# Where retention's weights begin in memory, and which raw tiles the pooling weights and the last gate rows take

## The chip, the core and the metric

The kernel runs on one core of a Trainium2 chip. The metric is the device time of one execution in microseconds (us). Three executions before the change took 2145.18, 2144.27 and 2141.74 us; the median is 2144.27 us.

The engines are named as the profile names them: PE is TensorE (PEld its loads of weights), DVE is VectorE, ACT is ScalarE, POOL is GpSimd, and SP is SyncE, which issues all but a few of this kernel's DMAs. A matrix product on PE has a stationary operand, the weights (128 columns loaded by one PEld instruction), and a moving operand that streams past them; the result goes to an accumulation bank.

## What is computed

One encoder layer on 1024 tokens of width 1024, in fp32: a SwiGLU block, a gated mixing layer, a second SwiGLU block. The change lies in the mixing layer:

```python
proj = rmsnorm(h) @ w_in            # q | k | v | g_ret | p_pool | gates
q, k = rotary(q), rotary(k) * 256 ** -0.5        # 4 heads of 256
scores = einsum("bnchd,bnshd->bnhcs", qc, kc) * inner_decay   # inside a chunk
inner  = einsum("bnhcs,bnshe->bnche", scores, vc)
cross  = (q_i * q_decay) @ state
state  = state * chunk_decay + (k_i * k_decay).T @ v_i
pooled = trailing_means(p) - p                   # windows 2, 4, 8, 16, one per group
mixed  = einsum("bsgc,gcd->bsgd", pooled, pool_w) * pool_scale
merged = sigmoid(gate0) * (ret @ w_ret_up) + sigmoid(gate1) * (mixed @ w_pool_up)
h = h + merged @ w_out
```

## The kernel before

**Products.** Every fp32 number is split into a high and a low part (`split`, L159: a CAST on ACT at L161 writes the high part, a TENSOR_TENSOR on DVE at L162 the low one; `split_scaled`, L164, does the same with a scale, at L165 and L166). A product is three matrix instructions (`mm3`, L179): high by high (L181), high by low (L182), low by high (L183). So PE runs in triples of lines L181, L182, L183. Most products stream 512 columns; the ones of retention stream 256.

**Order.** `Flow.run` (L62) calls `prep` of a step four steps ahead of its `body`, so loads and splits are written four steps ahead of the products that need them. A scheduler then orders the instructions of each engine by readiness and priority (`with soon()` raises it) and gives every tile a place in its ring; a tile that takes the place of an older one waits until that one has been read for the last time. Each engine, and SP as well, works off its own list in order: an instruction that waits holds up all behind it. The rings that matter here: `mv` (28 places of 4 KB per partition, split operands), `t4` (9 of 4 KB, long-lived tiles), `raw` (4 of 4 KB, weights as they come from memory), `c2` (8 of 2 KB, small results).

**Where weights begin.** `weights` writes the split weights into a `wt` tile (L111) that is 64 elements longer than needed, from element `at` on. The two SwiGLU blocks and the projections have one kind of product that streams 256 columns, that of two groups with blocks in common (`common`, L546); its weights are written from element `APART` = 22 on (L51, L553), which is byte 88 of 256, since tiles start at multiples of 256 bytes. All other weights begin at byte 0 of 256, those of retention too.

**Retention** works in 8 units of one head and one half of the tokens (`Unit`, L1455), named by two digits: unit 21 is head 2, second half. The stages and their names in a trace:

- `loads`: v, q, k from memory. `operands` splits q and k. For the last head `turn` rotates q and k on DVE just ahead.
- `keys` (`by_token`, L1432): PE turns the keys by token (transposes into a bank `kd..b`), and ACT and DVE scale and split them into `kd`, a tile of two parts per 256 tokens.
- `scores` (L1519): q by k into `s`, then DVE masks and scales into `sc`, and the split goes to `sm`.
- `updates`: `st` <- v by `kd`: the turned keys are the weights. Every unit with first half has two updates, with second half one.
- `products`: `ob` <- v by `sm` (`inner`, weights are the masked scores) and `ob` <- state by q (`across`, weights are q).
- `outputs`, `normalise`, `finish`: sums, scaling, PE turns the outputs (`ot`) and DVE multiplies them by the gate (`rg`); `ret` goes to memory.

**Fillers.** Between the stages of the units stand steps of the other branch, so that PE has work: `pool` (L1379) for the four groups, and `pool_up` (L1407) for eight blocks of 48 products of 512 columns. `pool` loads a group's weights into the first half of a raw tile (`pw`), splits them, and multiplies the pooled rows `pl` into `px`; the results are split into `po`. `pool_up` loads its weights into `pu..raw`, and at `begin` a row of gates into a raw tile `pg`; at the end DVE multiplies the bank by the gates in that tile (L1419) and SP stores it as `pm`. In the ring of raw tiles the loads therefore stand pu0raw, pg0, pu1raw, pg1 up to pu7raw, pg7, and then come those of the next stage.

**The next stage** (`merge`) begins with the product by w_ret_up in Strassen form, in pairs of groups: ru0 and ru1 first. A group loads two raw tiles, `ra` and `rb`; sums of their blocks (S1, S2 and so on; L455 on DVE) are split to weights `ru1wS` and multiplied by sums of `ret` (`ruR`, `ruT`). ru0a, ru1a, ru0b, ru1b are the groups' banks.

Of the kernel before, what the change touches and what calls it, by code (L numbers as in the profile page):

```python
# [17 lines left out]
P = 128  # L18
# [72 lines left out]
def block_kernel(ctx: ExitStack, tc, x, x_tok, vecs, f1_in, f1_out, w_in, w_v, pool_w, w_ret, w_pool, w_o,  # L91
# [28 lines left out]
    def raw(name):  # L120
        return sb.tile([P, S], F32, tag="raw", bufs=N_RAW, name=name)
# [17 lines left out]
    def load(dst, src):  # L139
        nc.sync.dma_start(dst, src)  # L140
# [8 lines left out]
    def half(t, j):  # L149
        return t[:, j * H : (j + 1) * H]  # L150
# [34 lines left out]
    def parts(m, at=slice(None)):  # L185
        return m[:, 0, at], m[:, 1, at]
# [1184 lines left out]
    def pooled_rows(n, i, first=False):  # L1371
# [4 lines left out]
        load(r, pooled[2 * n + i])  # L1376
        early[n, i] = [operand(half(r, j), f"{name}{j}") for j in range(2)]

    def pool(n):  # L1379
        Mg, w = {}, []  # L1380

        def prep():
            for i in range(2):
                if (n, i) not in early:
                    pooled_rows(n, i)
                Mg[i] = early[n, i]
            r = raw(f"pw{n}")
            load(half(r, 0), pool_w[n])
            w.append(weights(half(r, 0), f"pw{n}"))

        def body():
            for i in range(2):
                mt = 2 * n + i
                dst = [f(f"px{mt}{j}") for j, f in enumerate((sum_bank, bank))]
                for kt in range(2):
                    for j in range(2):
                        mm3(dst[j], parts(w[0], 2 * kt + i), parts(Mg[kt][j]), kt == 0, kt == 1)
                M[mt] = []
                for j in range(2):
                    m = mv(f"po{mt}{j}")  # L1400
                    with soon():
                        split_scaled(m[:, 0], m[:, 1], dst[j], vec[:, V_SCALE + mt : V_SCALE + mt + 1])
                    M[mt].append(m)

        return prep, body

    def pool_up():  # L1407
        gate = {}
        for mt in range(KT):

            def begin(mt=mt):
                gate[mt] = raw(f"pg{mt}")
                await_stored(f"t{(KT + mt) // 2}")
                load(gate[mt], gates[KT + mt])

            def evac(dst, mt=mt):
                gt = gate.pop(mt)
                for j in range(2):
                    tt(half(gt, j), dst[j], half(gt, j), MUL)  # L1419
                load(pm[mt], gt)  # L1420

            yield from plain(M.get, KT, w_pool[mt], f"pu{mt}", evac, begin,
                             (sum_bank, sum_bank if mt < 4 else bank))
# [5 lines left out]
        yield from pool_up()  # L1429


    def by_token(get, scale, name, n=2):  # L1432

        slots = []
        for jj in range(n):
            b = bank(f"{name}b{jj}")
            m = mv(f"{name}{jj}")
            for z in range(2):
                for i in range(2):
                    j = 2 * jj + z  # L1440
                    nc.tensor.transpose(b[:, z * HD + i * P : z * HD + (i + 1) * P], get(i)[:, j * P : (j + 1) * P],
                                        ident)
            for z in range(2):
                sl = slice(z * HD, (z + 1) * HD)
                with soon():
                    split_scaled(m[:, 0, sl], m[:, 1, sl], b[:, sl], scale(2 * jj + z))
            slots.append(m)
        return slots

    def col(t, n):  # L1450
# [2 lines left out]
    class Unit:  # L1453
# [65 lines left out]
        def scores(self):  # L1519

            self.sm = []
            for j in range(2):
                wid = SPAN - j * P
                b = bank(f"s{self.name}{j}")
                for s in range(2):
                    at, to = s * SPAN + j * P, b[:, s * SPAN : (s + 1) * SPAN]
                    for i in range(2):
                        w, m = parts(self.K[i], slice(at, at + P)), self.Q[i][:, :, at : at + wid]
                        first, final = s == 0 and i == 0, i == 1
                        if j == 0:  # L1530
                            mm3(to, w, (m[:, 0], m[:, 1]), first, final)
                        else:
                            mm(to, w[0], m, start=first, stop=False, skip_group_check=True)
                            mm(to[:, :P], w[1], m[:, 0], start=False, stop=final, skip_group_check=True)
                n = 2 * wid
                c = c2(f"sc{self.name}{j}")
                m = sb.tile([P, 2, H], F32R, tag="t4", bufs=N_T4, name=f"sm{self.name}{j}")
                with soon():
                    src = b
                    if j:  # L1540
                        both, src = b.rearrange("p (s z c) -> p s z c", s=2, z=2), c
                        sums = c[:, :n].rearrange("p (s c) -> p s c", s=2)
# [5 lines left out]
                    split(m[:, 0, :n], m[:, 1, :n], c[:, :n])  # L1548
                self.sm.append(m)

        def cell(self, b, t):
# [13 lines left out]
        def inner(self, s):  # L1565
            b, first = self.into(s)
            for j, t in ((0, 0), (0, 1), (1, 1)):
                at = s * (SPAN - j * P) + (t - j) * P

                mm3(self.cell(b, t), parts(self.sm[j], slice(at, at + P)), self.v(2 * s + j), first and t == 0, j == t)  # L1570

        def update(self, s):

            b = bank(f"st{self.name}{s}")
            for i in range(2):
                for j in range(2):
                    o = j * HD + i * P
                    mm3(b[:, i * HD : (i + 1) * HD], parts(self.kd[s], slice(o, o + P)), self.v(2 * s + j),
                        i == 0 and j == 0, j == 1)
# [410 lines left out]
```

## Time and profile before

| | |
|---|---|
| median of three executions | 2144.27 us |
| profiled execution, its own time | 2143.71 us |
| its span, first to last instruction | 2141.8 us |
| PE busy | 2129.9 us, 99% |
| PEld busy | 1809.6 us, 84% |
| DVE busy | 1874.0 us, 87% |
| ACT busy | 1103.3 us, 52% |
| granted TensorE clock | 1.0 in the whole span |

The profiled execution lies 0.56 us below the median; 1.9 us of its time are outside the span. Busy time is a sum over stages: what a change is worth has to be read in the stage where it acts, from which wait ends last there. A PE instruction's duration overlaps the next one's (they are pipelined), so what a matrix instruction costs PE is the distance from its start to the next start. For a wait the list of instructions in order of time shows the idle time ahead of an instruction in square brackets, with what ended it.

### The profile page before, as it was taken

How to read it: one execution, taken by the hardware profiler on the slowest of the kernel's cores; microseconds unless marked ns; L12 is line 12 of the kernel's file. 1: busy time of each engine (PE TensorE's matmuls, PEld its weight loads, DVE VectorE, ACT ScalarE, POOL GpSimd, SP SyncE). 2: the span in 40 equal slices, each digit the busy share in tenths (PEclk: the TensorE clock that was granted, in tenths of full speed). 3: DMA queues.
4: the chain of work that ended last, by engine and by line, in shares of the span. 5: the costliest groups of instructions: out<-in, count | busy, mean ns of one | idle time of the engine just before them, and what ended most of it. 6: DMA issues, size and time to landing. Idle time of an engine off the chain costs nothing.

```text
span 2141.8 us, 30121 instructions
## 1 busy us (share of the span) xinstructions
PE 2129.9 (99%) x10798; PEld 1809.6 (84%) x10798; DVE 1874.0 (87%) x3352; ACT 1103.3 (52%) x2082; POOL 0.2 (0%) x4
## 2 busy tenths in 40 slices
PE   9999999999999999999999999999999999999998
PEld 7888888888888888888888998788888888888887
DVE  8798898997986799999988888899988978899796
ACT  8544444554644544544457753456644544455454
POOL 0000000000000000000000000000000000000000
PEclk9999999999999999999999999999999999999999
DMA  7232323585543333233336567624133232358542
GB/s 259 75 133 74 138 84 130 200 275 178 173 142 94 109 121 115 106 122 109 119 128 227 196 203 262 220 89 163 64 105 117 90 123 84 131 199 275 192 138 99
DMA packets 116101, 313.59 MB, mean 146 GB/s; under 512 B 12784, under 2 KB 17008, under 8 KB 115952
## 3 DMA queue, kind: packets, MB, share of 16 engines
q1 hardware_dynamic: 115376, 310.63, 42.6%
q8 instruction: 84, 1.38, 0.3%
q10 hardware_dynamic: 576, 1.05, 0.1%
q14 instruction: 65, 0.53, 0.1%
HBM read 220.93 MB, written 90.70 MB: 145 GB/s over the span
## 4 chain that ended last, share of the span: by engine, by line
PE 91%; DVE 6%; DMA 1%; ACT 1%; issue 1%; SPq 0%; ACTq 0%; DVEq 0%
PE a_b L181 2%; PE a_b L182 2%; PE a_b L183 2%; PE c_b L181 2%; PE c_b L182 2%; PE c_b L183 2%; PE c_e L182 2%; PE c_e L181 2%; PE c_e L183 2%; PE a_e L181 2%; PE a_e L182 2%; PE a_e L183 2%; PE a_a L181 1%; PE a_a L183 1%; PE a_a L182 1%; PE c_a L181 1%
## 5 line engine op out<-in xcount | busy, mean ns | idle before, releaser
L182 PE MATMUL c_b<-n3T,c_wS 128*128 128x512 f32 x176 | 68.6, 390 | 0.0
L183 PE MATMUL c_b<-n3T,c_wS 128*128 128x512 f32 x176 | 68.5, 389 | 0.0
L181 PE MATMUL c_b<-n3T,c_wS 128*128 128x512 f32 x176 | 68.4, 390 | 0.0
L182 PE MATMUL a_b<-n1T,a_wS 128*128 128x512 f32 x168 | 65.4, 389 | 0.0
L181 PE MATMUL a_b<-n1T,a_wS 128*128 128x512 f32 x168 | 65.4, 389 | 0.0
L183 PE MATMUL a_b<-n1T,a_wS 128*128 128x512 f32 x168 | 65.3, 389 | 0.0
L181 PE MATMUL a_a<-n1R,a_wL 128*128 128x512 f32 x120 | 46.7, 389 | 0.0
L182 PE MATMUL a_a<-n1R,a_wL 128*128 128x512 f32 x120 | 46.7, 389 | 0.0
L183 PE MATMUL a_a<-n1R,a_wL 128*128 128x512 f32 x120 | 46.7, 389 | 0.0
L182 PE MATMUL c_a<-n3R,c_wL 128*128 128x512 f32 x112 | 43.6, 389 | 0.0
L181 PE MATMUL c_a<-n3R,c_wL 128*128 128x512 f32 x112 | 43.6, 389 | 0.0
L183 PE MATMUL c_a<-n3R,c_wL 128*128 128x512 f32 x112 | 43.6, 389 | 0.0
L183 PEld LDWEIGHTS c_b<-n3T,c_wS 128*128 128x128 f32 x176 | 33.0, 188 | 6.9
L182 PEld LDWEIGHTS c_b<-n3T,c_wS 128*128 128x128 f32 x176 | 33.0, 188 | 6.8 <-DVE n3T L162 0.2
L181 PEld LDWEIGHTS c_b<-n3T,c_wS 128*128 128x128 f32 x176 | 32.9, 188 | 6.9 <-ACT n3T L161 0.3
L162 DVE TENSOR_TENSOR a_wS<-a_S,a_wS 128x512 fp32r<-128x512 f32 x45 | 31.2, 695 | 8.0 <-ACT a_wS L161 8.0
L183 PEld LDWEIGHTS a_b<-n1T,a_wS 128*128 128x128 f32 x168 | 31.5, 188 | 6.6
L181 PEld LDWEIGHTS a_b<-n1T,a_wS 128*128 128x128 f32 x168 | 31.5, 188 | 6.4
L182 PEld LDWEIGHTS a_b<-n1T,a_wS 128*128 128x128 f32 x168 | 31.5, 188 | 6.4
L182 PE MATMUL c_e<-n3T,c_wL 128*128 128x512 f32 x88 | 34.5, 394 | 0.0
L161 ACT CAST c_wS<-c_S 128x512 fp32r<-128x512 f32 x46 | 28.0, 626 | 12.7 <-DVE c_S L455 7.1
L181 PE MATMUL c_e<-n3T,c_wS 128*128 128x512 f32 x88 | 34.4, 391 | 0.0
(3385 smaller groups left out, 8168.5 us busy)
## 6 DMA issues: line engine op xcount, KB each, us to landing
c_ra<-in_f_in SPq DMA_DIRECT2D x22, 512.0 KB, 3.7
c_rb<-in_f_in SPq DMA_DIRECT2D x22, 512.0 KB, 3.7
a_ra<-in_f_in SPq DMA_DIRECT2D x21, 512.0 KB, 3.8
a_rb<-in_f_in SPq DMA_DIRECT2D x21, 512.0 KB, 3.8
t<-au SPq DMA_DIRECT2D x11, 512.0 KB, 2.9
b<-ag SPq DMA_DIRECT2D x11, 512.0 KB, 4.1
r<-au SPq DMA_DIRECT2D x11, 512.0 KB, 3.8
bra<-in_f_out SPq DMA_DIRECT2D x11, 512.0 KB, 5.9
```

Source lines behind the costliest of these rows:

```text
L161: copy(hi, src)
L162: tt(lo, src, hi.bitcast(F32), SUB)
L181: mm(dst, w[0], m[0], start=start, stop=False, skip_group_check=True)
L182: mm(dst, w[0], m[1], start=False, stop=False, skip_group_check=True)
L183: mm(dst, w[1], m[0], start=False, stop=stop, skip_group_check=True)
```

## The change

Three edits; the number of matrix instructions and the arithmetic stay the same.

1. **Turned keys and masked scores begin at byte 88 of 256.** `keys` no longer takes a tile of two parts per 256 tokens. A new `pieces` takes whole tiles of 1024 elements, cuts three pieces of 256 elements from each, from element 22 on, and hands them out as high and low part in turn. `scores` takes two tiles at its start, one for high and one for low parts, and puts the scores of j = 0 at element 22 and those of j = 1 at element 22 + 512. So a first-half unit takes three tiles from `mv` for its keys instead of two, a second-half unit two instead of one; the scores take two from `t4` as before, but both at once.
2. **Pooled weights two to a raw tile.** For groups 0 and 2 `pool` loads the weights of two groups into the two halves of one tile; groups 1 and 3 take the second half.
3. **The last gate row in small tiles.** In `pool_up` the eighth row of gates goes to two `c2` tiles, by two loads of half the size, and is stored from there by two stores; the other seven stay in raw tiles.

```diff
+    blocks = {}
     def pool(n):
...
-            r = raw(f"pw{n}")
-            load(half(r, 0), pool_w[n])
-            w.append(weights(half(r, 0), f"pw{n}"))
+            if n % 2 == 0:
+                r = blocks["pw"] = raw(f"pw{n}")
+                for j in range(2):
+                    load(half(r, j), pool_w[n + j])
+            w.append(weights(half(blocks["pw"], n % 2), f"pw{n}"))
...
             def begin(mt=mt):
-                gate[mt] = raw(f"pg{mt}")
                 await_stored(f"t{(KT + mt) // 2}")
-                load(gate[mt], gates[KT + mt])
+                if mt < KT - 1:
+                    r = raw(f"pg{mt}")
+                    load(r, gates[KT + mt])
+                    gate[mt] = [half(r, j) for j in range(2)]
+                    stores[mt] = [(pm[mt], r)]
+                    return
+                gate[mt] = [c2(f"pg{mt}{j}") for j in range(2)]
+                for j, g in enumerate(gate[mt]):
+                    load(g, half(gates[KT + mt], j))
+                stores[mt] = [(half(pm[mt], j), g) for j, g in enumerate(gate[mt])]
...
+    def pieces(kind, n, name):
+        out = []
+        for k in range(-(-n // 3)):
+            m = kind(f"{name}{k}")
+            out += [m[:, APART + c * HD : APART + (c + 1) * HD] for c in range(3)]
+        return out[:n]
...
+    def operand_row(name):
+        return sb.tile([P, S], F32R, tag="mv", bufs=N_MV, name=name)
...
     def by_token(get, scale, name, n=2):
+        at = pieces(operand_row, 4 * n, name)
...
-                    split_scaled(m[:, 0, sl], m[:, 1, sl], b[:, sl], scale(2 * jj + z))
+                    split_scaled(hi, lo, b[:, sl], scale(2 * jj + z))
...
     def scores(self):
+            row = [sb.tile([P, S], F32R, tag="t4", bufs=N_T4, name=f"sm{self.name}{z}") for z in range(2)]
...
-                m = sb.tile([P, 2, H], F32R, tag="t4", bufs=N_T4, name=f"sm{self.name}{j}")
+                m = [x[:, APART + j * H : APART + j * H + n] for x in row]
```

`inner` and `update` take their weights from these pieces. With the tiles, the order of instructions on the engines moves, too. Three places follow; the names carry the program's buffer numbers, which differ between the two builds.

On SP, where the loads of the stage after retention begin, before:

```order
L140 DMA ru0rb_12994<-in_w_ret 128x1024
L140 DMA rg0_10_13172<-gt4_224 128x512
L140 DMA rg0_01_13288<-gt0_220 128x512
L140 DMA rg0_01_13288<-gt1_221 128x512
L140 DMA rg0_10_13172<-gt5_225 128x512
L140 DMA pm6_242<-pg6_12920 128x1024
L140 DMA ru1ra_13038<-in_w_ret 128x1024
L140 DMA pm7_243<-pg7_12964 128x1024
L140 DMA ru01_13164<-pm4_240 128x1024
L140 DMA ru1rb_13039<-in_w_ret 128x1024
```

The same place in the changed kernel:

```order
L140 DMA ru1ra_13046<-in_w_ret 128x1024
L140 DMA rg0_11_13178<-gt5_225 128x512
L140 DMA rg0_10_13181<-gt4_224 128x512
L140 DMA rg0_01_13297<-gt0_220 128x512
L140 DMA rg0_01_13297<-gt1_221 128x512
L140 DMA pm6_242<-pg6_12926 128x1024
L140 DMA rg0_10_13181<-gt5_225 128x512
L140 DMA ru1rb_13047<-in_w_ret 128x1024
L140 DMA pm7_243<-pg70_12970 128x512
L140 DMA pm7_243<-pg71_12971 128x512
```

Before, ru1rb stands behind the store pm7 of the last gate row, whose raw tile it takes over; now it stands ahead of that store and takes over the tile of pg6, while ru1ra takes that of pg5 and stands ahead of the store pm6.

On ACT, between the first scores and the first pooled results (`px` to `po`) of unit 00, before:

```order
L165 ACTIVATE po00_10989<-px00_10975,vec_66 128x512
L165 ACTIVATE po01_10992<-px01_10976,vec_66 128x512
L161 CAST pw2_11039<-pw2_11037 128x512
L165 ACTIVATE po10_11009<-px10_10995,vec_66 128x512
L161 CAST sm001_10943<-sc001_10942 128x256
L165 ACTIVATE po11_11012<-px11_10996,vec_66 128x512
```

In the changed kernel the casts of pw2 and pw3 stand some ten instructions earlier, and no cast is left between the four:

```order
L1198 ACTIVATE g2A_10725<-g2A_10725 128x1024
L161 CAST pw2_11040<-pw2_11037 128x512
L599 COPY g3A_10726<-g2x3_10815 128x256
L161 CAST pw3_11237<-pw2_11037 128x512
L1198 ACTIVATE g3B_10711<-g3B_10711 128x1024
```

Their load moved with them: on SP the two loads of pw2 stand right behind the loads of q01 and ahead of those of k01, where before the one load stood behind k01 and the stores g4 and g7.

On DVE, in unit 21, the changed kernel splits the second half of the weights of the fifth `pool_up` block between the first turned keys and the first scores:

```order
L166 SCALAR_TENSOR_TENSOR kd210_12178<-kd21b0_12180,by2_11815,kd210_12178 128x256
L162 TENSOR_TENSOR pu4w4_12707<-pu4raw_12625,pu4w4_12707 128x512
L1572 SCALAR_TENSOR_TENSOR sc210_12204<-s210_12191,by2_11815,dec2_11715 128x256
L166 SCALAR_TENSOR_TENSOR kd211_12179<-kd21b0_12180,by2_11815,kd210_12178 128x256
L1572 SCALAR_TENSOR_TENSOR sc210_12204<-s210_12191,by2_11815,dec2_11715 128x256
```

Before, this split stood two units later, behind the masked scores of unit 31 (L162 `sm311`).

More of the change, by code (lines that the diff above doesn't have):

```diff
@@ L1547, in scores @@
                         stt(c[:, at], src[:, at], self.row(8, 2 * s + j), self.dec[:, :wid], MUL, MUL)
-                    split(m[:, 0, :n], m[:, 1, :n], c[:, :n])
+                    split(m[0], m[1], c[:, :n])
                 self.sm.append(m)
@@ L1568, in inner @@
                 at = s * (SPAN - j * P) + (t - j) * P
-                mm3(self.cell(b, t), parts(self.sm[j], slice(at, at + P)), self.v(2 * s + j), first and t == 0, j == t)
+                mm3(self.cell(b, t), [x[:, at : at + P] for x in self.sm[j]], self.v(2 * s + j), first and t == 0, j == t)
         def update(self, s):
```

18 lines of the change are left out of this document (9 added, 9 removed).

## The prediction

> **What bounds the kernel now.** I read the page's busy shares first, then the clock, then the chain of waits.
>
> ```profile
> span 2141.8 us, 30121 instructions
> PE 2129.9 (99%) x10798; PEld 1809.6 (84%) x10798; DVE 1874.0 (87%) x3352; ACT 1103.3 (52%) x2082; POOL 0.2 (0%) x4
> PEclk9999999999999999999999999999999999999999
> PE 91%; DVE 6%; DMA 1%; ACT 1%; issue 1%; SPq 0%; ACTq 0%; DVEq 0%
> ```
>
> PE is busy 2129.9 of 2141.8 us at a full clock, and 91% of the chain that ends last is PE. So only two things can shorten the run: a shorter distance between matrix instructions, and the few places where PE stands idle. DVE, with 87%, is near enough to become the bound in a stretch. I took edit 1 by the distances and the other two by the waits.
>
> **Edit 1, the place of the weights.** It removes no instruction. It moves the weights of `st` (kd) and of `inner` (sm) from byte 0 to byte 88.
>
> ```profile
> L181 PE MATMUL st<-v,kd 128*128 128x256 f32 x48 | 13.6, 288 | 0.0
> L182 PE MATMUL ob<-v,sm 128*128 128x256 f32 x48 | 13.5, 283 | 0.0
> L183 PE MATMUL ob<-state,q 128*128 128x256 f32 x48 | 13.6, 283 | 0.0
> L183 PE MATMUL c_x<-n3R,c_wx 128*128 128x256 f32 x36 | 10.0, 278 | 0.0
> ```
>
> Each line of code stands 48 times for each product, so 3 x 48 x 2 = 288 matrix instructions move. The durations (288 and 283 against 278 for `c_x`, whose weights already begin at byte 88) overlap the next instruction, so they only hint at a difference. The price is the distance between starts, read from one unbroken run of each kind, first and last row:
>
> ```profile
> 1247.96 0.28 PE L181 MATMUL ob<-v,sm 128*128 128x256 f32 x1
> 1251.43 0.28 PE L183 MATMUL ob<-state,q 128*128 128x256 f32 x1
> 957.36 0.28 PE L181 MATMUL k1x<-n2R,k1wx 128*128 128x256 f32 x1
> 960.67 0.28 PE L183 MATMUL k1a<-n2R,k1ws 128*128 128x256 f32 x1
> ```
>
> ```profile
> 1247.95:1251.44 3.49, 3.49 (x31) 3.48 (x30) 3.49 (x9) 2.13 (x6) 0.00 (x0) 1.00 0.47 88
> 957.35:960.68 3.33, 3.33 (x31) 3.32 (x30) 1.98 (x4) 2.12 (x5) 0.00 (x0) 1.00 0.76 209
> ```
>
> The columns are length and then busy time (count) of PE, PEld, DVE, ACT and POOL. PEld shows 30 products in each (PE's 31st is the one before, still running), so 29 distances. At byte 0: (1251.43 - 1247.96) / 29 = 119.7 ns. At byte 88: (960.67 - 957.36) / 29 = 114.1 ns. Difference 5.6 ns, times 288 = 1.6 us. The first and last distance of a run hold some transition, and many distances inside lie nearer 120 and 113, which gives 7 x 288 = 2.0 us. I take **1.8 us**. The bounds: nothing, if the place isn't the cause (a rival below), and 2.0.
>
> A rule that speaks against term one: the Trainium skill, "TensorE: Matmul & The Clock Gate", Part 2, Step-by-step, says that TensorE reads weights and moving operand through two independent ports, that loading the next weights takes no bandwidth from the running product, and that loading time scales with columns alone. By it both runs should have one distance, and the edit would be worth 0; the 119.7 against 114.1 above, where nothing but operands differs, do not agree with it.
>
> What edit 1 costs: the splits that write to byte 88.
>
> ```profile
> L162 DVE TENSOR_TENSOR c_wS<-c_S,c_wS 128x512 fp32r<-128x512 f32 x46 | 32.0, 697 | 2.6 <-ACT c_wS L161 2.5
> L162 DVE TENSOR_TENSOR c_wx<-c_S,c_wx 128x512 fp32r<-128x512 f32 x10 | 7.0, 701 | 3.0 <-ACT c_wx L161 3.0
> ```
>
> 697 ns at byte 0, 701 at byte 88: 4 ns, on an engine with slack. No cost. The larger tiles in the ring `mv` are the slower rival below.
>
> **Edit 3, the last gate row.** PE's one long stop in the retention and pooling stretch is in ru1b:
>
> ```profile
> 1365.07 0.39 PE L181 MATMUL ru1b<-ruT,ru1wS 128*128 128x512 f32 x1
> 1365.30 0.39 PE L182 MATMUL ru1b<-ruT,ru1wS 128*128 128x512 f32 x1
> 1367.62 0.50 PE L183 MATMUL ru1b<-ruT,ru1wS 128*128 128x512 f32 x1 [1.94 <-DVE ru1wS L162]
> 1367.62 0.19 PEld L183 LDWEIGHTS ru1b<-ruT,ru1wS 128*128 128x128 f32 x1 [2.36 <-DVE ru1wS L162]
> ```
>
> L183 starts 2.32 us after the start before it, where the step before took 0.23. The chain back from there, in order of time:
>
> ```profile
> 1353.04 1.21 DVE pg L1419 x2
> 1354.27 2.59 DMA pm<-pg
> 1356.88 5.65 DMA ru1rb<-in_w_ret
> ```
>
> ru1rb takes the raw tile of the last gates, so its load waits for that row's product on DVE and its store on SP; DVE then stands idle until it lands. After the change ru1rb takes the tile of pg6. What that one does in the run before:
>
> ```profile
> 1341.53 1.28 DVE L1419 TENSOR_TENSOR pg<-pu6d,pg 128x512 f32<-128x512 f32 x2
> 1342.84 0.32 SPq L140 DMA_DIRECT2D pm<-pg  x1
> 1345.52 0.33 SPq L140 DMA_DIRECT2D ru1ra<-in_w_ret  x1
> 1349.32 0.62 ACT L161 CAST ru1wL<-ru1ra 128x512 fp32r<-128x512 f32 x1
> 1362.55 0.69 DVE L455 TENSOR_TENSOR ru1S<-ru1rb 128x512 f32<-128x512 f32 x1 [1.50 <-DMA ru1rb<-in_w_ret]
> ```
>
> pm6's store is issued at 1342.84 and the tile's next load, ru1ra, at 1345.52; its first reader runs at 1349.32. So ru1rb starts 1356.88 - 1345.52 = 11.4 us sooner; with the 5.65 us of the load in the chain it is in by 1351.2. DVE's 1.50 us idle then goes, and in its changed list ru1S stands ahead of the product with the last gates (1353.04), the split ru1wS2 some six instructions behind that product instead of nineteen. At the 0.6 us a row that DVE takes there, ru1wS2 is ready by about 1358, 7 us before PE asks for it at 1365. ru1ra, moved too, stands on SP ahead of pm6 and takes the earlier tile of pg5, so it can't be late either. Behind ru1rb on SP now waits the store of pm7, in two issues (another 0.32 us by the row of pm6), as the gates' load is; their readers come later than ru1b. Price: 2.32 - 0.23 = 2.1 us if the stop goes whole, 1.5 if only DVE's idle time does, 2.4 by PEld's own idle time (2.36 in its row of the same start). I take **2.2 us**, near the first. What is late next is another wait in ru0 and ru1 (rival two).
>
> **Edit 2, the pooled weights.**
>
> ```profile
> 1157.47 0.32 SPq L140 DMA_DIRECT2D k<-k  x1
> 1160.43 0.41 SPq L140 DMA_DIRECT2D pw<-in_pool_w  x1
> 1165.23 0.62 ACT L161 CAST pw<-pw 128x512 fp32r<-128x512 f32 x1 [1.20 <-DMA pw<-in_pool_w]
> 1166.47 1.64 DVE L166 SCALAR_TENSOR_TENSOR po<-px,vec,po 128x512 fp32r<-128x512 f32 x2
> 1167.28 0.19 PEld L181 LDWEIGHTS px<-pl,pw 128*128 128x128 f32 x1 [0.29 <-DVE po L166]
> 1168.16 0.19 PEld L181 LDWEIGHTS px<-pl,pw 128*128 128x128 f32 x1 [0.59 <-DVE po L166]
> 1169.09 0.19 PEld L182 LDWEIGHTS st<-v,kd 128*128 128x128 f32 x1 [0.64 <-DVE v L162]
> ```
>
> ACT stands 1.20 us for pw2, whose load is issued behind k's at 1157.47. After the change it is issued ahead of them, some 3 us sooner, with pw3's; k's loads fall behind by two issues, about 0.8 us. ACT's 1.20 vanish and both casts stand earlier. But the three idle times of PEld that follow (0.29 + 0.59 + 0.64 = 1.5 us) end with DVE, and DVE's rows there are close together. Bounds: 0, if DVE has no room, and 1.5, if it all stems from the late po. Nearest to DVE's rows is a third of ACT's delay: **0.4 us**.
>
> **What moves besides.** The split pu4w4 (one DVE instruction, 0.7 us by the row of c_wS) now stands in this stretch:
>
> ```profile
> 1258.00:1307.00 49.00, 48.79 (x321) 44.12 (x320) 48.57 (x101) 23.48 (x57) 0.00 (x0) 1.00 0.50 160
> 1262.37 0.19 PEld L183 LDWEIGHTS st<-v,kd 128*128 128x128 f32 x1 [0.27 <-DVE kd L166]
> ```
>
> DVE is busy 48.57 of 49.00 us, PE 48.79, and PE already waits now and then by 0.27. A 0.7 us instruction put in could cost 0.7; against it, some products of the next pool_up blocks now stand ahead of the scores of units 30 and 31 and fill PE. The list gives it back two units later. I take **0**, bounds 0.5 either way.
>
> **The sum.** -1.8 - 2.2 - 0.4 + 0 = -4.4 us. Against the profiled execution's own time (span 2141.8 plus the 1.9 around it = 2143.71) that is **2139.3 us**. The profiled execution lies 0.56 under the median 2144.27, so measured against the median the drop is 5.0 us or 0.23%. About 0.2% (4.3 us) is what a measurement of this kernel can tell from no change; the forecast sits at that edge.
>
> **Rivals.**
>
> *The place is not the cause.* For it: in this trace every 256-column product at byte 88 is one of a SwiGLU block or a projection, every one at byte 0 belongs to retention. Moving operand, neighbours and readers' traffic differ with the place, so 119.7 against 114.1 may come from v or the state instead. Against it: `inner` and `across`, with different weights and moving operands, have the same 283 ns. Then the change doesn't do what it says: -2.2 - 0.4 = -2.6, 2141.1 us.
>
> *Another wait takes the place of ru1rb's.* The two half loads of the last gates, the splits of ru0 or the moved ruT come late instead, and PE stops elsewhere in ru0 and ru1 for as long. For it: all of these are DVE's, and DVE does no less work than before. Against it: in the chain DVE's idle time there is put down to the one DMA, and 1.50 us of it come free. -1.8 - 0.4 = -2.2, 2141.5 us.
>
> *A row begun off the grid costs more.* A weight row at byte 88 doesn't begin where its 256-byte block does. If that costs what I think it saves, edit 1 is +1.6 and the sum -1.0: 2142.7 us. Against it stand all rows at byte 88, 114.1 ns. The Trainium skill, "SBUF — State Buffer", Specifications, gives cachelines of 16 bytes with a penalty at each cross to a new line; 88 is no multiple of 16, so a 512-byte row touches 33 lines instead of 32, by an estimate from that page 3% of 119.7 ns or 1.1 us in all; the trace's rows say the opposite.
>
> *Slower: the fuller ring.* A first-half unit takes three `mv` tiles instead of two, a second-half unit two instead of one, so the cast of a later k waits for a tile of older keys until `st` has read it.
>
> ```profile
> 1206.89 1.16 ACT L161 CAST k<-k 128x512 fp32r<-128x512 f32 x2
> 1209.05 0.28 PE L183 MATMUL st<-v,kd 128*128 128x256 f32 x1
> 1221.79 0.36 PE L181 MATMUL s<-q,k 128*128 128x256 f32 x1
> ```
>
> In unit 11 the second cast, begun at about 1207.4 (half of the pair's 1.16 us on), now needs the place of kd100, which the first update of unit 10 reads until 1209.05 + 0.28: a wait of 1.9 us on ACT. Queued behind it are ACT's other casts and scalings, for which PE and DVE wait. If it reaches PE in each of the 8 units: 8 x 1.9 = +15.2, less 4.4: 2154.5 us. It decides once a wait exceeds its cover. Here the scores that need k start at 1221.79, 12 us after that update, so the cover is six times the wait.
>
> **How the numbers follow.** Forecast 0.62 (own range 2138.3 to 2141.0), all gains at their upper end (-2.0 - 2.3 - 1.5 - 0.5 = -6.3, 2137.4) 0.05, place not the cause 0.15, another wait 0.10, off the grid 0.03, fuller ring 0.05. The range from 2137.0 to 2143.2 holds all but the fuller ring and a part of each side. Against the median, faster by over 0.2% means below 2140.0: two thirds of the forecast and the upper end, 0.46. Slower means above 2148.6: the fuller ring and a remainder, 0.06. Between: 0.48.
>
> **What the profile after would show.** Edit 1: the runs of `st` and of `inner` at 114 ns between starts, those of `across`, unchanged, still at 120. Edit 3: ru1rb's DMA near 1345, no 2 us stop in ru1b, and no DVE idle put down to it. Edit 2: no idle time of ACT for pw2, and PEld's three waits at 1167 to 1169 shorter. The ring: ACT waiting on PE ahead of k's cast in unit 11, and the first scores of that unit without a wait. The forecast is wrong if `inner` still runs at 120, if ru1b's stop moves to another weight of the pair, or if PE waits on ACT appear in several units.

## The result and the profile after

Over 21 executions of each kernel the median went from 2142.29 to **2139.57 us**; the ratio is 0.9985 with a 95% interval of 0.9979 to 0.9990, so 2 to 4.5 us faster, at the edge of what can be told from no change. One of the 21 executions after the change took 2656.88 us at a granted clock of 0.75 and is left out of the ratio. The forecast was 2139.3. The time came out, but not the drop: 2.7 us were measured against a sum of 4.4, and the kernel before had a median 2.0 us lower here than in its first three executions. The terms did not come out either, and the rest of this document is about that.

The page after, its first two lines and the chain's shares:

```profile
span 2138.8 us, 30140 instructions
PE 2128.6 (100%) x10798; PEld 1808.6 (85%) x10798; DVE 1873.7 (88%) x3352; ACT 1101.5 (52%) x2082; POOL 0.2 (0%) x4
PE 95%; DVE 3%; ACT 1%; DMA 0%; issue 0%; SPq 0%; DVEq 0%; ACTq 0%
```

PE's share of the chain rose from 91% to 95%, and the DMA's 1% is gone: ru1rb's load no longer stands in it. PE's busy time fell by 1.3 us with the same 10798 instructions.

**The weights.** The groups that answer to those of before (busy us and mean ns of one behind the first bar):

```profile
L182 PE MATMUL st<-v,kd 128*128 128x256 f32 x48 | 13.4, 280 | 0.2 <-DVE v L162 0.2
L182 PE MATMUL ob<-v,sm 128*128 128x256 f32 x48 | 13.3, 278 | 0.0
L183 PE MATMUL ob<-state,q 128*128 128x256 f32 x48 | 13.6, 283 | 0.0
L182 PEld LDWEIGHTS ob<-v,sm 128*128 128x128 f32 x48 | 9.0, 188 | 0.1
L183 PEld LDWEIGHTS ob<-state,q 128*128 128x128 f32 x48 | 9.2, 192 | 0.0
```

The two products that moved to byte 88 come down to 280 and 278 ns, where `c_x` stood before (278), and the scores' loads to 188 ns, as those of `c_x`. The product that stayed at byte 0 still has 283 and 192.

**The stop.** In ru1b the 2.1 us stop is gone (L181 to L182 below is 0.23 us, as in any row there). But ahead of it, in ru1a, there is a new one. From the list in order of time, of DVE, ACT and PE:

```profile
1352.31 0.69 DVE L455 TENSOR_TENSOR ru1S<-ru1rb 128x512 f32<-128x512 f32 x1 [0.57 <-DMA ru1rb<-in_w_ret]
1358.33 0.69 DVE L356 TENSOR_TENSOR ret<-ret,ret 128x512 f32<-128x512 f32 x1
1359.06 0.62 ACT L161 CAST ruT<-ret 128x512 fp32r<-128x512 f32 x1 [4.13 <-DVE ret L356]
1359.58 0.58 ACT L492 COPY ru1b<-ru1a 128x512 f32<-128x512 f32 x1
1360.21 0.50 PE L181 MATMUL ru1a<-ruR,ru1wL 128*128 128x512 f32 x1 [1.30 <-ACT ru1b L492]
1365.80 0.39 PE L181 MATMUL ru1b<-ruT,ru1wS 128*128 128x512 f32 x1
1366.03 0.39 PE L182 MATMUL ru1b<-ruT,ru1wS 128*128 128x512 f32 x1
```

Since ru1rb is there early, DVE's list has the work on it ahead of the differences of `ret` (L356). On ACT a cast of such a difference stands ahead of the copy of ru1a's bank. The cast waits 4.13 us, the copy waits behind it, and PE may write that bank again only after the copy. The cast makes T4, which the pair's last product alone needs: something nobody waits for held up something that PE waited for.

**Where the time went, by stage.** The profiled executions stand at 2143.71 us (before) and 2141.33 us (after); both are above their medians. Two other profiles, of the same two kernels (e9 and e7 below), are nearer to them, at 2141.93 and 2139.07 us. The stages are cut at the starts of the last products into `g3e`, `ob` and `ru1b`; the rows of e9 and then of e7 that cut the second:

```profile
1156.64 0.39 PE L183 MATMUL g3e<-n2T,g3wL 128*128 128x512 f32 x1
1311.48 0.28 PE L183 MATMUL ob<-state,q 128*128 128x256 f32 x1
1390.34 0.39 PE L183 MATMUL ru1b<-ruR,ru1wS 128*128 128x512 f32 x1
```

```profile
1156.41 0.39 PE L183 MATMUL g3e<-n2T,g3wL 128*128 128x512 f32 x1
1309.76 0.28 PE L183 MATMUL ob<-state,q 128*128 128x256 f32 x1
1387.92 0.39 PE L183 MATMUL ru1b<-ruR,ru1wS 128*128 128x512 f32 x1
```

| us | start to g3e | g3e to ob (retention) | ob to ru1b | ru1b to end | span |
|---|---|---|---|---|---|
| before, three profiles | 1156.57, .64, .70 | 154.89, 154.84, 154.70 | 80.13, 78.86, 78.17 | 750.2, 749.7, 749.3 | 2141.8, 2140.0, 2138.9 |
| after, two profiles | 1157.26, 1156.41 | 153.33, 153.35 | 79.47, 78.16 | 748.7, 749.4 | 2138.8, 2137.3 |
| e7 less e9 | -0.23 | -1.49 | -0.70 | -0.32 | -2.74 |

Only the retention stage differs by the same amount whichever profiles are compared: -1.4 to -1.6 us. The stage from `ob` to `ru1b`, where the larger term was forecast, spreads by 2 us before and 1.3 us after from one execution to the next. The two stages at the ends add up to 0.1 to 1.0 us less after the change, depending on the profiles compared; among the three profiles of before alone they differ by 0.7. Behind `ru1b` PE's order is the same in both kernels. Yet with edit 1 or 3 in the kernel that last stage takes 748.6 to 749.0 us in all profiles but e7, and without them 749.3 to 750.2; why was not settled.

### The profile page after: what moved, and what is told of

The parts are those of the page before. It is cut to its first block, busy times and chain, and to the rows that moved or that the text cites. A ratio compares the mean times of both kernels' runs of the same rounds, so it can differ in the third digit from the quotient of the medians.

```text
span 2138.8 us, 30140 instructions
## 1 busy us (share of the span) xinstructions
PE 2128.6 (100%) x10798; PEld 1808.6 (85%) x10798; DVE 1873.7 (88%) x3352; ACT 1101.5 (52%) x2082; POOL 0.2 (0%) x4
## 4 chain that ended last, share of the span: by engine, by line
PE 95%; DVE 3%; ACT 1%; DMA 0%; issue 0%; SPq 0%; DVEq 0%; ACTq 0%
PE c_b L181 2%; PE c_b L182 2%; PE c_b L183 2%; PE a_b L181 2%; PE a_b L182 2%; PE a_b L183 2%; PE c_e L182 2%; PE c_e L181 2%; PE c_e L183 2%; PE a_e L181 2%; PE a_e L182 2%; PE a_e L183 2%; PE a_a L181 1%; PE a_a L183 1%; PE a_a L182 1%; PE c_a L181 1%
## 5 line engine op out<-in xcount | busy, mean ns | idle before, releaser
L182 PE MATMUL c_b<-n3T,c_wS 128*128 128x512 f32 x176 | 68.6, 390 | 0.0
L181 PE MATMUL c_b<-n3T,c_wS 128*128 128x512 f32 x176 | 68.4, 390 | 0.0
L182 PE MATMUL a_b<-n1T,a_wS 128*128 128x512 f32 x168 | 65.4, 389 | 0.0
L181 PE MATMUL a_b<-n1T,a_wS 128*128 128x512 f32 x168 | 65.4, 389 | 0.0
L181 PE MATMUL a_a<-n1R,a_wL 128*128 128x512 f32 x120 | 46.7, 389 | 0.0
L182 PE MATMUL a_a<-n1R,a_wL 128*128 128x512 f32 x120 | 46.7, 389 | 0.0
L182 PE MATMUL c_a<-n3R,c_wL 128*128 128x512 f32 x112 | 43.6, 389 | 0.0
L181 PE MATMUL c_a<-n3R,c_wL 128*128 128x512 f32 x112 | 43.6, 389 | 0.0
L182 PEld LDWEIGHTS c_b<-n3T,c_wS 128*128 128x128 f32 x176 | 33.0, 188 | 6.8 <-DVE n3T L162 0.2
L181 PEld LDWEIGHTS c_b<-n3T,c_wS 128*128 128x128 f32 x176 | 33.0, 188 | 6.8 <-ACT n3T L161 0.3
L181 PEld LDWEIGHTS a_b<-n1T,a_wS 128*128 128x128 f32 x168 | 31.5, 188 | 6.4
L182 PEld LDWEIGHTS a_b<-n1T,a_wS 128*128 128x128 f32 x168 | 31.5, 188 | 6.4
L162 DVE TENSOR_TENSOR a_wS<-a_S,a_wS 128x512 fp32r<-128x512 f32 x45 | 31.1, 693 | 6.6 <-ACT a_wS L161 6.5
L182 PE MATMUL c_e<-n3T,c_wL 128*128 128x512 f32 x88 | 34.5, 393 | 0.0
L181 PE MATMUL c_e<-n3T,c_wS 128*128 128x512 f32 x88 | 34.4, 391 | 0.0
```

The lines of the kernel that those rows point to most:

```text
L162: tt(lo, src, hi.bitcast(F32), SUB)
L181: mm(dst, w[0], m[0], start=start, stop=False, skip_group_check=True)
L182: mm(dst, w[0], m[1], start=False, stop=False, skip_group_check=True)
```

## The experiments

Theory: the place of the weights sets the distance between starts, and edit 3 takes a wait for a raw tile away, part of which comes back through ACT's list. Rivals: the distance belongs to retention's products; the stop is DVE's and only moves; the ring `mv` becomes the bound.

**e4: the changed kernel with the pieces begun at byte 0.** The order of instructions on every engine is that of the changed kernel; addresses alone differ.

```diff
-            out += [m[:, APART + c * HD : APART + (c + 1) * HD] for c in range(3)]
+            out += [m[:, c * HD : (c + 1) * HD] for c in range(3)]
...
-                m = [x[:, APART + j * H : APART + j * H + n] for x in row]
+                m = [x[:, j * H : j * H + n] for x in row]
```

> The changed kernel with the same tiles and pieces, but the first piece at element 0 instead of 22, in keys and in scores: all five engines' lists are those of the changed kernel, word for word, and only the addresses differ. Theory (the place): st and the scores' products are back at 120 ns a start, 1.6 to 2.0 us slower than the changed kernel, so 0.7 to 1.6 us faster than before. Rival (the distance comes from other tiles, neighbours or order): 114 ns as in the changed kernel and no difference from it, about 2.7 to 3.2 us faster than before.

Its groups:

```profile
L182 PE MATMUL st<-v,kd 128*128 128x256 f32 x48 | 13.6, 284 | 0.2 <-DVE v L162 0.2
L182 PE MATMUL ob<-v,sm 128*128 128x256 f32 x48 | 13.5, 283 | 0.0
L182 PEld LDWEIGHTS ob<-v,sm 128*128 128x128 f32 x48 | 9.2, 192 | 0.1
```

284, 283 and 192: those of before, in the changed kernel's tiles and order. So for these products the place is the cause, and the rival that the distance belongs to retention is out. How much it is worth comes out in two ways. Over the starts within a run (those up to 130 ns apart, nearly all of the 144 of each kind), the mean distance goes from 119.3 to 115.8 ns for the keys and from 119.9 to 115.4 for the scores; times 144 each that is 0.50 + 0.65 = 1.15 us. The retention stage, cut in e4 at these two rows, is 153.87 us against 153.34 in the changed kernel, 0.5 us apart:

```profile
1157.69 0.39 PE L183 MATMUL g3e<-n2T,g3wL 128*128 128x512 f32 x1
1311.57 0.28 PE L183 MATMUL ob<-state,q 128*128 128x256 f32 x1
```

One reason that the stage gains less than the distances is that e4 doesn't show a wait of 0.36 us at the pooled rows that the changed kernel has. And e4's stage, with its weights at byte 0, is itself 0.8 to 1.0 us shorter than the three of before. So of the 1.5 us that retention gained, about a third shows as the place of the weights and two thirds as the moved order; what moved is told below, under DVE's full stretch. The time was 2140.5 us, 2.0 below the kernel before beside it where 0.7 to 1.6 had been expected; the ratio, 0.9994 (0.9985 to 1.0003), is told neither from the changed kernel's nor from 1.

**e1 and e11: edit 1 alone**, twice (the diff's parts in `pieces`, `by_token`, `scores`, `inner` and `update`).

> The kernel before with edit 1 alone: turned keys and masked scores begin at byte 88; pool weights and the last gate row as before. Theory (the place of the weights sets the distance): the runs of st and of the scores' products go from 120 to 114 ns a start, the state's products stay at 120, 288 x 5.6 to 7 ns = 1.6 to 2.0 us faster than before; ru1b's stop of 2.3 us stays, since the last gates still hold the raw tile that ru1rb needs, and the ACT copy of ru1a's bank stands behind three casts as before. Rival (the distance belongs to the products of retention, not to the place): 120 ns everywhere and no change in time. Rival (the fuller ring): ACT waits ahead of the casts of k in several units and the time is over that of before.

> Edit 1 alone once more, for its profile. Its eleven times fell in two groups, five from 2139.1 to 2140.2 and six from 2142.9 to 2145.6 us, while the three kernels with edit 3 had all but a few of theirs within 2 us. Theory (what edit 3 takes away is a stop that comes long in some executions): where the time is in the upper group, the stop at ru1b is 2 us or more longer than the 1.2 us of the first profile; where it is in the lower group, the stop is as short as there. Rival (the two groups come from elsewhere): the stop does not go with the time.

e1: 2142.91 us, ratio 1.0000 (0.9991 to 1.0009): no change that the times can tell, though they leave room for 1.9 us either way. Its retention stage is 153.1 us, in e11 153.3, so 1.4 to 1.8 us shorter than before. In the profiles ob to ru1b takes a part of that back: 79.35 and 80.28 us against the 77.9 that the stage takes without a stop. PE comes there earlier, the raw tile doesn't. Both kinds of stop stand in e11:

```profile
1359.40 0.50 PE L181 MATMUL ru1a<-ruR,ru1wL 128*128 128x512 f32 x1 [1.04 <-ACT ru1b L492]
1366.39 0.50 PE L183 MATMUL ru1b<-ruT,ru1wS 128*128 128x512 f32 x1 [0.77 <-DVE ru1wS L162]
```

Counted by starts they cost 1.20 + 0.94 us in e11, whose time was 2141.17; in e1's profile 0.20 + 1.02 at 2140.22. The stops differ by 0.92, the times by 0.95 us. The stop at ru1a is there without edit 3, so edit 3 alone doesn't make it. The copy that PE waits for comes no sooner in e1 than in the kernel before (here before, then e1):

```profile
1357.81 0.58 ACT L492 COPY ru1b<-ru1a 128x512 f32<-128x512 f32 x1
1357.78 0.58 ACT L492 COPY ru1b<-ru1a 128x512 f32<-128x512 f32 x1
```

PE, with retention shorter, starts the product ahead of the stop at 1357.99 instead of 1359.41 us, and so meets a copy that used to be done by then. That the upper of the two groups of times (2142.9 and above) has longer stops still was not seen: neither profile fell in it. The wait that the slower rival spoke of shows in e11 and in e12, once each. From the list in e11 of who waited for whom between 1165 and 1312 us (us in total, times, longest):

```profile
ACT k L161 <- PE st L182: 0.7, 1, 0.7
PEld s L183 <- DVE k L162: 0.2, 1, 0.2
```

ACT's cast of `k` waits 0.7 us for `st`. The scores behind it wait for `k` no more than the 0.2 us that they had before: the cover holds.

**e3: edit 3 alone.**

> The kernel before with edit 3 alone: the last gate row in two small tiles. In its list on ACT the copy of ru1a's bank stands ahead of all four casts of T4 (ruT from ret), where in the changed kernel one of them stands ahead of it. Theory (what gave back 1.5 us of edit 3 in the changed kernel is that one cast ahead of the copy): ru1b's stop of 2.3 us is gone and no stop of over 0.5 us is put in ru1a; about 2.1 us faster than before. Rival (DVE has no more room, so the stop only moves): a stop of 1 to 2 us at ru1a's second product or later in the pair; 0.5 to 1 us faster than before.

2139.88 us, ratio 0.9985 (0.9976 to 0.9993): as much as the whole change. No stop of over 0.15 us is left in ru0 and ru1, and ob to ru1b takes 77.86 us, 0.3 to 2.3 less than the three profiles of before. The rival that DVE has no room is out: it is busy without a gap there, and still in time.

**e5: the changed kernel with T4 later.** **e7: the changed kernel beside it.**

```diff
-            up.work(up.r22, up.t2, up.t1, up.t3, up.r21, up.p22, up.t4_)
+            up.work(up.r22, up.t2, up.t1, up.t3, up.r21, up.p22)
+            flow.add(*[none] * 8)
+            up.work(up.t4_)
```

> The changed kernel with the four steps that make T4 (differences of ret, then casts) queued eight steps later: on ACT the copy of ru1a's bank stands ahead of all T4 casts; T4 is needed by the last product of the pair alone. Theory (the copy waits behind a cast that waits for DVE): ACT's wait of 4.1 us for ret and PE's stop of 1.46 us at ru1a's second product go; about 1.4 us faster than the changed kernel, 4.1 to 4.6 us faster than before. Rival (DVE is full there, and another wait takes the place): PE stops elsewhere in ru0 or ru1 for as long, and the time is that of the changed kernel within 0.5 us.

> The changed kernel itself, beside the one with T4 later, on the same chip: 2.7 to 3.2 us faster than before, the stop of about 1.5 us at ru1a's second product again, at the same instruction. If the stop is chance, it is absent or of another length.

In e5's list the copy comes as soon as PE is done, and PE goes on without a bracket:

```profile
1356.21 0.57 ACT L492 COPY ru1b<-ru1a 128x512 f32<-128x512 f32 x1 [1.61 <-PE ru1a L183]
1358.73 0.39 PE L181 MATMUL ru1a<-ruR,ru1wL 128*128 128x512 f32 x1
1359.82 1.22 ACT L161 CAST ruT<-ret 128x512 fp32r<-128x512 f32 x2 [2.50 <-DVE ret L356]
```

The cast still waits 2.50 us for `ret`, but stands behind the copy. ob to ru1b takes 77.86 us, exactly e3's. e5 ran in 2139.12 us, the changed kernel beside it in 2139.74: 0.6 us apart, with intervals that overlap, where 1.4 had been expected. A reason shows in e7's own profile:

```profile
1350.20 0.69 DVE L455 TENSOR_TENSOR ru1S<-ru1rb 128x512 f32<-128x512 f32 x1
1356.94 0.62 ACT L161 CAST ruT<-ret 128x512 fp32r<-128x512 f32 x1 [3.16 <-DVE ret L356]
1357.46 0.58 ACT L492 COPY ru1b<-ru1a 128x512 f32<-128x512 f32 x1
```

The same order, and the cast ahead of the copy again, but DVE has no wait for ru1rb, and all three rows come 2.1 us earlier. The stop at ru1a is 0.19 us here, was 1.46 in the first profile and 0.65 in e4, which has the same order. So the wait is there in all of them, and its length goes with the execution.

**e9 and e10: the kernel before, twice more.** Same program as in the prediction.

> The kernel before once more, for its profile. In the profiles without edit 3 so far the stop at ru1b was 2.1 us (before), 1.2 in two pieces (edit 1 alone) and under 0.15 (edit 2 alone), with ru1rb's load in at 1362.5, about 1361.0 and 1360.6. Theory (the stop is as long as the chain of the two transfers happens to be in that execution): a stop of another length, that follows the landing of ru1rb at one to one. Rival (the stop is part of the kernel's order, and the other edits shorten it): 2.0 to 2.2 us again.

> The kernel before a third time, as e9: by the theory a stop of between 0 and over 2 us that differs from the other two by the landing of ru1rb; by the rival 2.0 to 2.2 us.

The chain of e9 at the place quoted in the prediction, and PE's row of the stop in e9:

```profile
1354.29 2.59 DMA pm<-pg
1356.89 4.39 DMA ru1rb<-in_w_ret
1361.30 0.70 DVE ru1S L455
```

```profile
1365.31 0.39 PE L182 MATMUL ru1b<-ruT,ru1wS 128*128 128x512 f32 x1
1366.38 0.50 PE L183 MATMUL ru1b<-ruT,ru1wS 128*128 128x512 f32 x1 [0.68 <-DVE ru1wS L162]
```

And in e10, DVE's row and PE's two:

```profile
1360.55 0.69 DVE L455 TENSOR_TENSOR ru1S<-ru1rb 128x512 f32<-128x512 f32 x1
1365.24 0.39 PE L182 MATMUL ru1b<-ruT,ru1wS 128*128 128x512 f32 x1
1365.62 0.50 PE L183 MATMUL ru1b<-ruT,ru1wS 128*128 128x512 f32 x1
```

The store and the issue of the load are the same to 0.02 us in the first profile and in e9; the load of 512 KB took 5.65 us in one and 4.39 in the other. ru1S follows at 1362.55, 1361.30 and 1360.55, the start in ru1b at 1367.62, 1366.38 and 1365.62, and the stop over a plain step of 0.23 is 2.1, 0.85 and 0.15 us: one to one. The theory of a stop that varies holds; in e10 DVE doesn't wait for the load at all, and nearly no stop is left. Two thirds of e10's lead over e9 come from ahead of the load, which was issued at 1356.39; it took 4.13 us. In the three profiles with edit 1 or 2 alone the load took 4.19 to 4.48, so the 5.65 of the first profile, on which the prediction rests, is the longest of six.

**e2: edit 2 alone.**

> The kernel before with edit 2 alone: pooled weights two to a raw tile. Theory, as the changed kernel's trace suggests (PE's waits near 1165 to 1170 add up to 0.7 us there, as before): no gain, within 0.2 us of before in that stretch. Rival, the prediction's term: 0.4 us faster, PEld's waits at 1167 to 1169 shorter. Either is within the noise of the times, so the trace decides.

2141.22 us, ratio 0.9995 (0.9986 to 1.0004). The retention stage is 155.08 us, 0.2 to 0.4 longer than before. Before, PE waits among the pooled products at the start at 1168.16 that the prediction shows; the changed kernel (first) and e2 wait earlier:

```profile
1164.41 0.47 PE L181 MATMUL px<-pl,pw 128*128 128x512 f32 x1 [0.20 <-DVE g3A L1158]
```

```profile
1164.38 0.47 PE L181 MATMUL px<-pl,pw 128*128 128x512 f32 x1 [0.31 <-DVE g3A L1158]
```

By starts these waits are 0.32 us before, then 0.36 and 0.47. ACT's wait for the pooled weights went from 1.20 to 0.56 us (0.73 in e2), where the prediction had none left; in e3, without edit 2, it is 0.76. PE's wait went to an earlier product, where DVE is behind by another instruction.

**e6: a place for each unit.** The changed kernel with 16 places, one for each unit's keys and one for its scores:

```diff
+AT = {'kd00': 0, 'kd01': 4, 'kd10': 8, ... 'sm00': 48, 'sm01': 56, ... 'sm31': 60}
...
-            out += [m[:, APART + c * HD : APART + (c + 1) * HD] for c in range(3)]
+            a = AT[name]
+            out += [m[:, a + c * HD : a + (c + 1) * HD] for c in range(3)]
...
-                m = [x[:, APART + j * H : APART + j * H + n] for x in row]
+                a = AT[f"sm{self.name}"]
+                m = [x[:, a + j * H : a + j * H + n] for x in row]
```

> The changed kernel with another first element for each unit's keys and scores: keys of units 00 to 31 at bytes 0, 16, 32, 64, 88, 96, 128, 160 of 256, scores at bytes 192, 224, 48, 80, 112, 8, 176, 240. One look, read by the distances between starts in each run. If any place off the start of 256 bytes will do, all are at 114 ns but byte 0. If it goes by a smaller grid (32 or 64 bytes), the multiples of it are at 120 and the rest at 114. If the distance is a property of 88 or of its neighbourhood alone, few are at 114. A place that starts within a 16-byte line (8, 88) and costs more would speak for a price by lines touched.

One profile, span 2138.65 us. Loads of weights split cleanly. At byte 0 (keys of unit 00, and q) a load takes 190 to 192 ns in the median of most runs; at each of the other fifteen places 187 to 189. The scores, which are nowhere at byte 0 in this kernel, have the figure of the changed kernel (all lines are one higher here):

```profile
L184 PEld LDWEIGHTS ob<-state,q 128*128 128x128 f32 x48 | 9.2, 191 | 0.0
L184 PEld LDWEIGHTS ob<-v,sm 128*128 128x128 f32 x48 | 9.0, 188 | 0.0
```

So for the load any place off the start will do, byte 8 as well as 88 or 128. The distances between starts do not split so: 113 ns on the mean at byte 192, 116 at 8, 117 to nearly 120 at the thirteen others, 119 to 120 at 0. So a load of 188 ns doesn't by itself bring the shorter distance. None of the expectations fits that, and place and unit can't be told apart in this run. Nor does it show a price for starting within a 16-byte line: bytes 8 and 88 are among the better ones.

**e8: the scores' products first.** e5 with this in `products`:

```diff
+            for s in range(2):
+                self.inner(s)
             if self.nh == 1:
                 self.across(0, self.state)
-            for s in range(2):
-                self.inner(s)
             self.across(1, self.mid)
```

> The changed kernel with T4 later, and in the units of the second half the scores' products (weights at byte 88) ahead of the first product with the state (weights q, at byte 0) instead of behind it. In the changed kernel a run at byte 88 goes at 113 to 114 ns where it follows 512-column products, and at 116.7 where it follows a 256-column run at byte 0. Theory (a run keeps the pace in which it was entered): the scores' runs of units 11, 21 and 31, which now follow 512-column products, go at 114 ns, and 0.2 us are gained in all, too little for the times. Rival (the second half's own tiles set 116.7): they stay at 116.7 ns.

The first and last of the 18 starts with the scores of unit 11, in the changed kernel and in e8:

```profile
1232.81 0.28 PE L181 MATMUL ob<-v,sm 128*128 128x256 f32 x1
1234.79 0.28 PE L183 MATMUL ob<-v,sm 128*128 128x256 f32 x1
```

```profile
1230.60 0.28 PE L181 MATMUL ob<-v,sm 128*128 128x256 f32 x1
1232.54 0.28 PE L183 MATMUL ob<-v,sm 128*128 128x256 f32 x1
```

1.98 us over 17 steps is 116.5 ns, 1.94 is 114.1. Units 21 and 31 do the same (116.7 to 114.5 in finer figures of all three). The tiles didn't change, only what runs ahead: 512-column products instead of a 256-column run at byte 0. So what runs ahead decides here, as if a run at byte 88 kept the pace in which it is entered, 113 to 114 or nearly 117. The order of instructions alone doesn't set the pace everywhere: the 21 starts of unit 00's first keys go at 113.8 ns in the changed kernel's first profile and at 116.7 in e7's, the same program. Median 2138.80 us, ratio 0.9984 (0.9974 to 0.9994).

**e12: e8 without edit 2.** Pooled weights one to a raw tile, as before.

> The kernel of e8 (the changed one, T4 later, the scores' products ahead of the state's in the second half) without edit 2: pooled weights one to a raw tile again. Theory (edit 2 costs what it should gain: with it the stretch from the last gate product to the last product of retention is 0.3 us longer in the profile of edit 2 alone than in three of before): that stretch, 153.3 us in e8, is 152.9 to 153.1 us here, and the time 2.8 to 4 us below before, not to be told from e8's 3.0. Rival (the prediction's term, edit 2 gains 0.4 us by the wait for the pooled weights): the stretch is 153.5 us or longer.

The stage is 153.22 us against 153.30: neither the theory's 152.9 to 153.1 nor the rival's 153.5. With edit 2 the stage is longer by 0.1 us here and by 0.2 to 0.4 in e2, where the three profiles of before differ by 0.2 among themselves. A gain of 0.4 is not seen; whether there is a loss stays open. 2138.66 us, ratio 0.9986 (0.9977 to 0.9995). With e8 that is the lowest median, but the kernel before was lower beside these two as well (2141.84 and 2141.85 us), and their ratios are no better than the changed kernel's 0.9985 and 0.9984. The stops at ru1a and ru1b are gone in e3, e5, e8 and e12 (ob to ru1b 77.86 us in each); a gain over the changed kernel is not shown by the times.

## Why the prediction was right, and which steps of it were not

The time fell within the forecast's own range, and both main mechanisms were at work. That the number came so close is luck in part: the drop was 2.7 us instead of 4.4, and the kernel before was lower by 2.0 us than in its first three executions.

**The weights: right in mechanism, mis-sized.** Forecast 1.8 us, measured 1.15 by the distances of e4 and the changed kernel, 0.5 by the stage. The step that failed is "119.7 against 114.1, times 288": it took the distance of a SwiGLU run for all of retention's. Most runs entered behind a 256-column run at byte 0, or behind the first scores, go at 117 instead of 114. For the first kind e8 shows that in three units. About 3 to 3.3 ns on some half of the 288 is the missing 0.5 us or so. The rule of the Trainium skill that the prediction weighed, by which loading time goes by columns alone, is off here by 4 ns: e4 and the changed kernel have the same lists, 192 against 188 ns a load and 119.9 against 115.4 a start. Whether a load takes anything from the running product, these runs do not tell.

**The raw tile: right in mechanism, sized from one execution.** Forecast 2.2 us, taken from a stop of 2.1 in the one profile there was. Three profiles have 2.1, 0.85 and 0.15, as the load came in later or sooner; by stages the wait is worth 0.3 to 2.3 us. The step that failed is the sum against the profiled execution's own time: a row of 5.65 us for a DMA was read as its price, though it was one draw. The early load was not issued near 1345 either, but at 1347.88 and, in e7, 1346.69 us: the store of pm6 ahead of it took 3.31 and 3.75 us instead of 2.66. In the first profile DVE still waited 0.57 us for the load.

**"Another wait in ru0 and ru1"** was given one chance in ten, as a rival that would cost the whole 2.2. It came, but as a part: 0.19 to 1.46 us at ru1a, by the copy behind the cast on ACT. The argument against it, that DVE's idle time comes free, was true for the most part and beside the point. The engine whose list decided was ACT, which the prediction did not follow past the new place of ru1S. Nor did it ask what the shorter retention does there: e1 and e11 have the stop at ru1a with edit 1 alone.

**The pooled weights:** forecast 0.4, measured between nothing and a loss of 0.4. The bound of nothing, "if DVE has no room", is nearest to what the profiles show.

**DVE's full stretch:** forecast 0, bounds 0.5 either way. The moved order was worth 0.8 to 1.0 us by e4's stage, over the bound, on the good side. The forecast followed the split pu4w4; what counted is the second split of the keys. In the kernel before, PE's loads for `st` wait for it in units 11 and 21 (us in total, times, longest):

```profile
PEld st L183 <- DVE kd L166: 0.5, 2, 0.3
```

DVE has two masked scores ahead of that split in unit 11 there, and in e4 one:

```profile
1223.64 0.88 DVE L1547 SCALAR_TENSOR_TENSOR sc<-s,by,dec 128x256 f32<-128x256 f32 x2
1224.42 0.49 DVE L166 SCALAR_TENSOR_TENSOR kd<-kd11b,by,kd 128x256 fp32r<-128x256 f32 x1
```

```profile
1224.58 0.47 DVE L1572 SCALAR_TENSOR_TENSOR sc<-s,by,dec 128x256 f32<-128x256 f32 x1
1224.97 0.47 DVE L166 SCALAR_TENSOR_TENSOR kd<-kd11b,by,kd 128x256 fp32r<-128x256 f32 x1
```

The wait is gone in e4, in the changed kernel and in e1, and stands in e2 and e3, so it goes with edit 1. With a stop of 0.3 us in unit 31 ahead of the scores, which goes too, it makes the 0.3 us by which e4 is shorter than before in each of the units 11, 21 and 31.

**The slower rivals** did not come: the ring's wait was 0.7 us, once in e11 and once in e12, and was not seen to reach PE, and places off the grid cost nothing.

In sum, of the 2.7 us between e9 and e7 some 1.5 lie in retention (by e4 about 0.5 from the weights and 1.0 from the moved order), 0.7 in ru0 and ru1, and 0.5 in the stages at both ends. The forecast had 1.8, 2.2 and 0.4.

## What to carry to other kernels

A wait behind a DMA has the length of that DMA in that execution. Before a stop is priced from a single profile, take a second and third of the same kernel: here a stop was 2.1, 0.85 and 0.15 us, and with edit 3 alone the times were narrower (all eleven within 2 us) as well as lower. When a transfer comes early, follow what it lets ahead on each engine in turn, to the first instruction that waits in order with something PE needs behind it. And to price an address, compare kernels with equal lists that differ in it alone.

## What the runs showed of the hardware

Where a product streams 256 columns, weights that begin at byte 0 of 256 load in 192 ns and at any of fifteen other places in 187 to 189, and such products at byte 0 start every 120 ns. The address alone doesn't do it: in the kernel before, weights of products that stream 512 columns begin at byte 0 as well and load in 188 ns.

```profile
L183 PEld LDWEIGHTS c_a<-n3R,c_wL 128*128 128x128 f32 x112 | 21.0, 188 | 4.4
```

At byte 88 the 256-column products go every 113 to 114 ns or every 117; which of the two is set at least in part by what ran ahead (e8: 116.5 to 114.1 with the same tiles). At the other places, each seen in one unit of one run, they go every 113 to nearly 120. Why a run keeps its pace was not settled, nor whether the pattern repeats every 256 bytes.

One load of 512 KB from memory, issued in the same program at the same time to 0.02 us, took 5.65 us in one execution and 4.39 in another.
